# Earlier query loads, spaced recurrence loads and an earlier closing in a two-layer block

## Chip, core and metric

The kernel runs on one core of a Trainium2 chip. The metric is device time in microseconds for one execution of the whole program, about 92,000 instructions, of which one part is changed here.

## What is computed

A first block (gated delta rule beside a dilated attention, then a feed-forward part) gives x. Then two layers of a second block follow, on 256 context rows and 1024 rows of x, 1280 in all, with 1024 channels. A layer is, cut to what matters:

```python
h = x * (1 + scale) + shift                       # context rows have their own scale and shift
u, gates, q, k, v, nq, nk, nv = split(h @ w_in)
# recurrence: six heads of 64 x 64 state, one pass forward and one backward over the rows
S = S * w - (S @ kk) b^T + v k^T ;  y = S @ r
yr = group_norm(y_f + y_b) + bonus
ya = softmax(q k^T) v                             # six query heads on two key heads, all 1280 keys
yn = softmax([nq nk_window^T + bias, nq nk_ctx^T]) [nv_window, nv_ctx]     # four heads, local
x = layer_norm(alpha * x + gate * (concat(yr, ya, yn) * silu(gates)) @ w_out)
```

In the first layer the context rows are updated as well; in the last they aren't, so the attentions and the closing product have 8 tiles of 128 rows instead of 10. Products in the dense parts are made of three fp32r matmuls of high and low halves (L243 to L245).

## The kernel before

A layer has four parts: `front` (projections and the recurrence's factors), `stage` (the recurrence, both attentions and the gates' product), `finish` (closing product with w_out2, residual and layer norm), and the transposes for the next layer. The change lies in `stage` and `finish`.

In `stage` the order of work on TensorE, VectorE, ScalarE and GpSimd is written out by a planner, `Timeline`, and fixed in `tc.manual_schedule` for these four engines. Each stream of work is a generator. It yields a phase ("-" for work off TensorE; "F", "V", "B", "Q" for matmuls of one kind), a delay, the time from which it may go on, and the PSUM places that it wants. `Timeline.spend` adds up estimated durations, a DMA at 2 us plus its bytes; `run` takes, at each step, the stream that is due, smaller rank first. SP, whose queue issues all loads and stores, isn't among the engines of the manual schedule: its order is made by the scheduler, which issues a load once its buffer is free. On every engine instructions run in the order of its queue.

The streams of the stage:

- `scan` (rank 0): ten steps of the recurrence, each of two sub-steps with four products, each sub-step waiting for the one before. It needs the three preparations of its step. After a step it calls `launch(s + 2)`.
- `prep` (rank 1 + s * 0.05), one for each step and pair of heads, thirty a layer. It takes one of four tickets, loads `bk` (2 DMAs), `G` and `SK` (4 each), multiplies, then solves a triangular system in `tri_inverse2`: a small tensor `wC` goes out to `wD` (L423), comes back copied over the partitions as `wR` (L425, 512 KB), GpSimd runs 30 short instructions on it (L436, L438) and TensorE finishes (L449 to L485).
- `end` (rank 2): group norm of a finished pair of row blocks, and the store to `ydr` (L2022). The blocks of step 9 are the outermost of the sequence, those of step 6 the innermost (tiles 5 and 6).
- the attentions (ranks 3 and 4): `jobs` yields one job for a tile of 128 queries and a pair of heads, 30 + 20 of them in layer 0 and 24 + 16 in layer 1. For each, `query` loads four pieces of 32 KB into `qraw` (L2059, one buffer), casts them on ScalarE to `qst` (L2101) and subtracts on VectorE (L2104). Then `scores` multiplies (L687) and drains each bank on VectorE (L691), `soft` exponentiates (L648), `values` transposes (L723), copies (L727) and multiplies (L744), `put` stores.
- the gates' product ahead of them, tiles `gth` and `go` (L1538 to L1540).

`stage` runs the planner until all ends are done (`done.done`) and the third set of keys is there. Then the two pools on the right, E and W, which hold the recurrence's tiles and y, are closed, and `Closing` opens pools there. `Closing.loads` brings w_out2 in eight pieces (L2214), each cast on ScalarE (L2221) and subtracted on VectorE or GpSimd (L2223). The planner then runs dry. `finish` goes over the tiles in order; for each it loads the gates and `ydr`, multiplies (L2248), splits into `yh` and `yl` (L153, L154), multiplies with the weights (L243 to L245) and makes the norm.

Of the kernel before, what the change touches and what calls it, by code (L numbers as in the profile page):

```python
# [71 lines left out]
    return c  # L72


ALONE = {"a": FULL[2] + FULL[1] + FULL[0], "t": FULL[3] + FULL[5] + FULL[6], "pv": FULL[4] + FULL[7]}


class K:
# [547 lines left out]
def attend_rounds(k, rounds, wk, jobs, width, bufs):  # L626
# [7 lines left out]

    def load():
        for job in jobs(state):
            if isinstance(job, str):
                yield job
                continue
            loaded.append(job)  # L640
            state.todo += 1
            while loaded:
                yield WAIT
        state.more = False
# [117 lines left out]
D = 1024  # L762
# [536 lines left out]
D = 1024  # L1299
# [209 lines left out]
def gates(k, tl, I, l, last, dn, sets, cols, gp, hT, L):  # L1509

    nc = k.nc
    state = type("State", (), {"sets": 0, "done": False})()

    def weights():
        for i in (2, 3):
            sets.append((yield from dn.steps(cols(i), eng=nc.vector, go=lambda: state.sets > i - 2)))

    def products():
        for j in range(8):
            while len(sets) <= j // 2:  # L1520
                yield WAIT
            hi, lo = sets[j // 2]
            c = slice(j % 2 * 128, j % 2 * 128 + 128)
            for t0, n in LAT if last else SEG:
                for a in (0, 4):
                    yield "F", 0.0, 0.0, () if a else ("a",)
                    if a == 0:
                        p = k.bank([128, 512], "a")[:, :n]
                    else:
                        tl.used.append(k.places["a"][(k.turn["a"] - 1) % len(k.places["a"])])  # L1530
                    for kk in range(a, a + 4):
                        h, m = hT.at(kk, t0, n)
                        nc.tensor.matmul(p, lhsT=hi[:, kk, c], rhs=h, start=kk == 0, stop=False)
                        nc.tensor.matmul(p, lhsT=hi[:, kk, c], rhs=m, start=False, stop=False)
                        nc.tensor.matmul(p, lhsT=lo[:, kk, c], rhs=h, start=False, stop=kk == 7)
                th = gp.tile([128, 512], F32, tag="gth", name="gth", bufs=2)[:, :n]
                o = gp.tile([128, 512], F32, tag="go", name="go", bufs=2)[:, :n]
                nc.scalar.activation(th, p, AF.Tanh, scale=0.5)  # L1538
                nc.vector.scalar_tensor_tensor(o, th, 1.0, p, ALU.add, ALU.mult)
                nc.sync.dma_start(L.gates[:, j, t0:t0 + n], o)  # L1540
            state.sets = (j + 1) // 2
        state.done = True

    return weights(), products(), state


# [262 lines left out]
class Homes:  # L1809
# [3 lines left out]
    FIRST = {"SK00", "SK01", "G00", "G01", "AB0", "betok0", "wF0", "wS", "wC"} | {  # L1813
        f"{nm}{i}" for nm in ("bk", "A", "wB", "wR", "wX16", "wY16") for i in range(2)}

    def __init__(self, first):
        self.first, self.last = first, None

    def tile(self, shape, dtype, tag, name, bufs=1):
        return (self.first if tag in self.FIRST else self.last).tile(shape, dtype, tag=tag, name=name, bufs=bufs)  # L1820


def rwkv(k, rounds, wk, l, last, L):
# [42 lines left out]
    def prep(s, pr):  # L1866
        a = s % NS
        f, b = fwd[s], bwd[s]
        sk, g = SK[a], G[a]
        while not tickets:  # L1870
            yield WAIT
        ticket = tickets.pop(0)
# [40 lines left out]
    def scan():  # L1913
        for s in range(10):
# [69 lines left out]
            if want(s) and not first(s):  # L1984
                o = y.pop(group(s))
                for pr in range(3):
                    rounds.add(end(o[:, pr], pr, group(s)), 2, ended)

    def blocks(ap, g):

# [32 lines left out]

    done = [0] * 10
    tickets = [0, 1]
    state = type("State", (), {"ends": 0, "done": False})()

    def ended(_):
        state.ends += 1
# [22 lines left out]
def attention(k, rounds, I, kp, gp, l, last, L):  # L2052
# [20 lines left out]
    have = type("State", (), {"keys": 0})()  # L2073
    early = gp.tile([128, 2, NT], F32, name="early")
    for h in range(2):
        both(early[:, h], sets[0][h])
# [1 line left out]
    def keys(n):  # L2078
# [12 lines left out]
            yield "-"  # L2091
        have.keys += 1

    def query(srcs):

        raw = wk.tile([128, 2, 128], F32, tag="qraw", name="qraw", bufs=1)
        for h, src in enumerate(srcs):
            both(raw[:, h], src)
        yield "-"
        q = wk.tile([128, 2, 128], F32R, tag="qst", name="qst", bufs=3)  # L2100
        nc.scalar.copy(q, raw)  # L2101
        yield "-"
        lo = slice(64, 128)
        nc.vector.tensor_tensor(q[lo], raw[lo], q[lo].bitcast(F32), ALU.subtract)  # L2104
        yield "-"
        return q

# [1 line left out]
        return lambda h, a, n: [(q[:, h], t[:, first + a:first + a + n]) for t in KT[h]]  # L2109

    def put(j, ts_):
        return lambda yo: nc.sync.dma_start(L.ydr[:, j, ts_], yo)

    def tiles():
        for t in range(2 if last else 0, 10):
# [2 lines left out]
    def jobs(state):  # L2118
        def values(c0):
            v = wk.tile([128, 10, 128], F32, tag="nav", name="nav", bufs=2)  # L2120
            nc.sync.dma_start(v, L.nv[:, :, c0:c0 + 128])
            return v

        v = values(0)

        rounds.read()
        rounds.landed = 0.0
        for j in range(3):
            for t, ts_ in tiles():
                nk = NT if t >= 2 else CTX  # L2130
                q = yield from query([L.gqk[h * 64:h * 64 + 64, j, ts_] for h in range(2)])
                yield ([(nk, score(q), None)],
                       [(b * 128, lambda h, b=b, v=v: v[:, b, h * 64:h * 64 + 64]) for b in range(nk // 128)],
                       put(3 + j, ts_))
        for p in range(2):
# [10 lines left out]
            for t, ts_ in tiles():  # L2146
                if t >= 2:
# [13 lines left out]
                q = yield from query([L.nqk[h * 64:h * 64 + 64, p, ts_] for h in range(2)])  # L2161
# [31 lines left out]
class Closing:  # L2193


    def __init__(self, k, tc, I, l):
        self.pools = ExitStack()
        self.wr, self.wa, self.wb = (self.pools.enter_context(
            tc.tile_pool(name=f"{n}{l}", bufs=1, reuse_waits="tile", side="right")) for n in ("fr", "fa", "fb"))
        self.dn, self.ws = Dense(k, [self.wa, self.wb, self.wb, self.wb], self.wr, raws=2), [None] * 4  # L2200
        self.ap = I["w_out2"][l]

    def loads(self):
# [15 lines left out]
        for n, (i, a) in enumerate(parts):  # L2219
# [4 lines left out]
            if n < 4:  # L2224
                fetch()


def finish(k, tc, I, l, last, L, M, src, dst, done, cl):

    nc = k.nc  # L2230
    pool = lambda name, side: tc.tile_pool(name=f"{name}{l}", bufs=1, reuse_waits="tile", side=side)
    with cl.pools, pool("fy", "right") as wy, pool("fo", "left") as wk:
        dn, ws = cl.dn, cl.ws
        rows = None
        gate = wy.tile([128, 2, D], F32, name="gaterows")
        for v in range(2):
            nc.sync.dma_start(gate[:, v], M.gate[l][v:v + 1].to_broadcast([128, D]))
        for t in range(2 if last else 0, 10):
            ts_ = slice(t * 128, t * 128 + 128)

            y = []
            for o, e in ((3, 8), (0, 3)):
                n = e - o
                yr = wy.tile([128, n, 128], F32, tag=f"yr{o}", name="yr", bufs=2)
                gt = wy.tile([128, n, 128], F32, tag=f"gt{o}", name="gt", bufs=1)
                nc.sync.dma_start(gt, L.gates[:, o:e, ts_])
                nc.sync.dma_start(yr, L.ydr[:, o:e, ts_])
                nc.vector.scalar_tensor_tensor(yr, yr, 0.5, gt, ALU.mult, ALU.mult)  # L2248
                yh = wy.tile([128, n, 128], F32R, tag=f"yh{o}", name="yh", bufs=2)
                yl = wy.tile([128, n, 128], F32R, tag=f"yl{o}", name="yl", bufs=2)  # L2250
                k.split(yh, yl, yr)
                y.append((o, n, yh, yl))
# [91 lines left out]
def stage(k, tc, I, l, last, dn, hT, hps, L, weights):  # L2344
# [6 lines left out]
    with second:  # L2351
        ep = second.enter_context(pool("E", "right"))
        with ExitStack() as st:
            dn = Dense(k, [st.enter_context(pool(n, "right")) for n in ("ga", "gb")], st.enter_context(pool("gr", "right")), raws=2)
            cols = lambda i: [(I["w_in2"][l][:, 2688 + i * 256:2944 + i * 256], 0)]
            sets = [dn.load(cols(i), eng=nc.vector) for i in range(2)]
            k.places = SECOND
            gp = st.enter_context(pool("GT", "right"))
            man = tc.manual_schedule(engines={e.engine for e in (nc.tensor, nc.vector, nc.scalar, nc.gpsimd)})
            man.__enter__()  # L2360
            tl, homes = Timeline(k), Homes(ep)
            loads, products, gate = gates(k, tl, I, l, last, dn, sets, cols, gp, hT, L)
# [6 lines left out]
            ap = hps.enter_context(pool("A", "left"))  # L2369
            convert(ap)  # L2370
        homes.last = second.enter_context(pool("W", "right"))
        attend()
        go()
        tl.run(lambda: done.done and have.keys == 3)
    k.places = ALONE
    cl = Closing(k, tc, I, l)
    tl.add(cl.loads(), 8)
    tl.run()
    tl.close()
    man.__exit__(None, None, None)  # L2380
# [174 lines left out]
```

## Time and profile before

| | us |
|---|---|
| median of 3 runs | 4414.95 (4407.27 to 4433.86) |
| the profiled execution | 4414.57 |
| its span, first to last instruction | 4412.8 |
| TensorE busy | 3949.0 (89%) |
| GpSimd busy | 1699.5 (39%) |
| VectorE busy | 2166.8 (49%) |
| ScalarE busy | 1448.3 (33%) |

The page gives the busy time of each engine; the windows view gives it for a stretch, with the clock that TensorE was granted in it (1.00 is full speed) and the share of the 16 DMA engines. The waits view names for each waiting line the line that released it last. A row of the timeline is one instruction, or several alike, with the idle time of its engine just before it and what ended that. Where a short instruction waits in an engine's queue, all behind it wait too, so the name at the end of a wait is often not its cause.

### The profile page before, as it was taken

What the parts mean: (1) busy time and instruction counts of PE and PEld (TensorE: products, weight loads), DVE (VectorE), ACT (ScalarE), POOL (GpSimd) and SP (SyncE); (2) the same over time, 40 slices, a digit from 0 to 9 for tenths busy, and PEclk for the clock granted to TensorE, in tenths of its full rate; (3) what the DMA queues carried; (4) which work ended last, traced back from release to release, by engine and by line L of the source; (5) the groups of instructions that cost most, each with busy time, mean ns of one, the idle gap of its engine ahead of it and who ended that gap; (6) DMA issues with size and microseconds to landing.
All of it is one profiled execution on the core that took longest, in us unless ns stands there. A gap on an engine that the chain in (4) does not pass through costs nothing. (4 is left out here: it accounts for less than half of the span.)

```text
span 4412.8 us, 91628 instructions
## 1 busy us (share of the span) xinstructions
PE 3949.0 (89%) x36914; PEld 3200.0 (73%) x36914; DVE 2166.8 (49%) x4701; ACT 1448.3 (33%) x2831; POOL 1699.5 (39%) x3201
## 2 busy tenths in 40 slices
PE   8989998989999989899869898988989987898878
PEld 6767777967888867578747776778767866676658
DVE  5633332499221155664235555557566424554546
ACT  4244443321111132221125554442222114554341
POOL 2444333433232254342223444336444224434424
PEclk9999999999999989889979999999889998999889
DMA  3343224354111133453232334354345333324434
GB/s 112 117 131 88 82 74 131 127 162 151 44 46 50 43 120 114 152 179 95 81 102 63 74 73 109 91 157 144 114 156 177 104 98 81 76 64 100 100 111 138
DMA packets 523961, 466.87 MB, mean 106 GB/s; under 512 B 66416, under 2 KB 448656, under 8 KB 523408
## 3 DMA queue, kind: packets, MB, share of 16 engines
q1 hardware_dynamic: 523536, 461.02, 35.7%
q8 instruction: 289, 4.73, 0.4%
q14 instruction: 136, 1.11, 0.1%
HBM read 330.43 MB, written 130.43 MB: 104 GB/s over the span
## 5 line engine op out<-in xcount | busy, mean ns | idle before, releaser
L154 POOL TENSOR_TENSOR wlo<-wraw,whi 128x1024 fp32r<-128x1024 f32 (+3 forms) x134 | 318.9, 2395 | 565.1 <-ACT whi L153 513.1
L436 POOL TENSOR_TENSOR wY<-wR,wX 128x60 f32<-128x60 f32 (+5 forms) x900 | 233.3, 259 | 405.2 <-DMA wR<-wD 353.0
L153 ACT CAST whi<-wraw 128x1024 fp32r<-128x1024 f32 (+3 forms) x164 | 156.9, 989 | 372.5 <-PE bank L245 162.8
L691 DVE CUSTOM_DVE_ANT_0 S<-bank,zero 128x256 f32<-128x256 f32 (+1 forms) x372 | 204.5, 558 | 151.4 <-PE bank L687 149.4
L245 PE MATMUL bank<-h2T,wlo 128*128 128x512 f32 x704 | 278.5, 397 | 0.0
L244 PE MATMUL bank<-h2T,whi 128*128 128x512 f32 x704 | 278.0, 395 | 0.0
L243 PE MATMUL bank<-h2T,whi 128*128 128x512 f32 x704 | 275.6, 394 | 0.3 <-ACT h2T L785 0.3
L727 ACT COPY PT<-bank 128x512 f32<-128x512 f32 x346 | 201.7, 584 | 222.4 <-PE bank L723 221.6
L243 PE MATMUL bank<-whi,yh 128*128 128x256 f32 x832 | 240.5, 289 | 31.7 <-ACT yh L153 31.7
L438 POOL TENSOR_TENSOR wX<-wX,wY 128x60 f32<-128x60 f32 (+5 forms) x900 | 239.1, 266 | 70.5
L723 PE MATMUL bank<-cst,S 128*128 128x128 f32 x1416 | 238.4, 292 | 23.5 <-ACT PT L727 14.6
L744 PE MATMUL bank<-PT,nav 128*64 128x128 f32 (+1 forms) x2832 | 242.8, 294 | 16.5 <-ACT PT L727 16.1
L245 PE MATMUL bank<-whi,yl 128*128 128x256 f32 x832 | 238.9, 288 | 0.5 <-POOL yl L154 0.5
L244 PE MATMUL bank<-wlo,yh 128*128 128x256 f32 x832 | 239.2, 288 | 0.0
L744 PEld LDWEIGHTS bank<-PT,nav 128*64 128x64 f32 (+1 forms) x2832 | 154.4, 141 | 86.8 <-issue 55.3
L415 POOL TENSOR_TENSOR wB<-A,cst 128x256 f32<-128x256 f32 x60 | 45.2, 753 | 446.6 <-DVE A L1889 446.5
L723 PEld LDWEIGHTS bank<-cst,S 128*128 128x128 f32 x1416 | 164.1, 146 | 62.8 <-ACT PT L727 26.2
L648 ACT ACTIVATE S<-S,mx 128x1280 f32<-128x1280 f32 (+3 forms) x180 | 202.7, 1127 | 9.1 <-DVE mx L695 6.4
L243 PE MATMUL bank<-hT,whi 128*128 128x512 f32 x464 | 190.4, 410 | 9.1 <-ACT sqkv L131 6.7
L244 PE MATMUL bank<-hT,whi 128*128 128x512 f32 x464 | 187.3, 404 | 0.0
L243 PEld LDWEIGHTS bank<-whi,yh 128*128 128x128 f32 x832 | 162.5, 195 | 33.2 <-ACT yh L153 32.9
L245 PE MATMUL bank<-hT,wlo 128*128 128x512 f32 x464 | 186.2, 402 | 0.0
(467 smaller groups left out, 10919.3 us busy)
## 6 DMA issues: line engine op xcount, KB each, us to landing
wraw<-in_w_in SPq DMA_DIRECT2D x86, 512.0 KB
wR<-wD SPq DMA_DIRECT2D x60, 512.0 KB
wm<-in_w_mod SPq DMA_DIRECT2D x96, 256.0 KB
X<-R SPq DMA_DIRECT2D x12, 1280.0 KB
G<-gt SPq DMA_DIRECT2D x24, 640.0 KB
bk<-bk SPq DMA_DIRECT2D x24, 640.0 KB
bk<-bk SPq DMA_DIRECT2D x120, 128.0 KB
G<-G SPq DMA_DIRECT2D x240, 64.0 KB
```

What stands on the lines that cost most here:

```text
L153: self.nc.scalar.copy(hi, raw)
L154: (eng or self.nc.gpsimd).tensor_tensor(lo, raw, hi.bitcast(F32), ALU.subtract)
L243: nc.tensor.matmul(p, lhsT=lh, rhs=rh, start=kk == 0, stop=False)
L244: nc.tensor.matmul(p, lhsT=lh, rhs=rl, start=False, stop=False)
L245: nc.tensor.matmul(p, lhsT=ll, rhs=rh, start=False, stop=kk == n - 1)
L436: eng.tensor_tensor(t, custom(R, i * 64 + i + 1, [((15 - 2 * i) * 64 + 31 - i, 2), (16, 2), (1, n)]), custom(x, i, [(47 - 2 * i, 2), (16, ...
L438: eng.tensor_tensor(o, o, t, ALU.subtract)
L648: nc.scalar.activation(s[:, :total], s[:, :total], AF.Exp, bias=mx[:, 5:6], accum_out=mx[:, 6:7])
L691: nc.vector.tensor_tensor_reduce(out=s[:, c0:c0 + n], in0=p[:, c0 % 512:c0 % 512 + n], in1=b, scale=1.0, scalar=-3.0e38, op0=ALU.add, op1= ...
L723: nc.tensor.transpose(pt[:rows[i], i], P[h][0][:, c0:c0 + rows[i]], k.ident)
L727: nc.scalar.copy(t[:, :full], pt[:, :full])
L744: nc.tensor.matmul(pv[h * 64:h * 64 + 64, 0], lhsT=V, rhs=t[:V.shape[0], i], start=seen[h] == 1, stop=seen[h] == n)
```

## The change

- `query` no longer loads. `sources` lists all query tiles of the layer in the order of the jobs; `ask` loads the next one into `qraw`, which has two buffers, and notes when the planner takes it to have landed. Two are asked for at the start; each query asks for the next but one after its subtraction. The first queries of the second attention are so asked for ahead of its keys.
- `prep` of steps 1 to 9 yields a delay of 5 us times the number of its pair before it takes a ticket and loads.
- The planner's first run ends when the last scan has been placed (`done.scanned`) and the third set of keys is there, not when all ends are. The tiles `y`, `vv`, `gsq` and `hrs` move to the pool A on the left, which stays open; E and W are closed with ends still to come. `ALONE` gives up bank 0, and stands beside `SECOND` from then on.
- When the ends are done and the last attention has stored its first 2 (layer 0) or 5 (layer 1) tiles, the gates and `ydr` of the first two tiles of the closing are loaded, multiplied and split inside the stage (`Closing.first`, rank 7). The last layer's closing takes its tiles in the order 5, 6, 4, 7, 3, 8, 2, 9.
- The gates' tanh is written where the result goes; `go` has three buffers, `gth` is gone.

```diff
-ALONE = {"a": FULL[2] + FULL[1] + FULL[0], "t": FULL[3] + FULL[5] + FULL[6], "pv": FULL[4] + FULL[7]}
+ALONE = {"a": FULL[2] + FULL[1], "t": FULL[3] + FULL[5] + FULL[6], "pv": FULL[4] + FULL[7]}
...
-                th = gp.tile([128, 512], F32, tag="gth", name="gth", bufs=2)[:, :n]
-                o = gp.tile([128, 512], F32, tag="go", name="go", bufs=2)[:, :n]
-                nc.scalar.activation(th, p, AF.Tanh, scale=0.5)
-                nc.vector.scalar_tensor_tensor(o, th, 1.0, p, ALU.add, ALU.mult)
+                o = gp.tile([128, 512], F32, tag="go", name="go", bufs=3)[:, :n]
+                nc.scalar.activation(o, p, AF.Tanh, scale=0.5)
+                nc.vector.scalar_tensor_tensor(o, o, 1.0, p, ALU.add, ALU.mult)
...
+    ENDS = {"y", "vv", "gsq", "hrs"}
...
+        pool = self.first if tag in self.FIRST else self.ends if tag in self.ENDS else self.last
...
         sk, g = SK[a], G[a]
+        if s:
+            yield "-", 5.0 * pr
         while not tickets:
             yield WAIT
...
+        state.scanned = True
...
+    asked = []
+
+    def sources():
+        for src, j in [(L.gqk, j) for j in range(3)] + [(L.nqk, p) for p in range(2)]:
+            for _, ts_ in tiles():
+                yield [src[h * 64:h * 64 + 64, j, ts_] for h in range(2)]
+
+    def ask(srcs):
+
+        src = next(srcs, None)
+        if src is None:
+            return
+        raw = wk.tile([128, 2, 128], F32, tag="qraw", name="qraw", bufs=2)
+        rounds.read()
+        landed, rounds.landed = rounds.landed, 0.0
+        for h in range(2):
+            both(raw[:, h], src[h])
+        rounds.read()
+        asked.append((raw, rounds.landed))
+        rounds.landed = landed
+
     def query(srcs):
 
-        raw = wk.tile([128, 2, 128], F32, tag="qraw", name="qraw", bufs=1)
-        for h, src in enumerate(srcs):
-            both(raw[:, h], src)
-        yield "-"
+        raw, landed = asked.pop(0)
+        yield "-", 0.0, landed
         q = wk.tile([128, 2, 128], F32R, tag="qst", name="qst", bufs=3)
         nc.scalar.copy(q, raw)
         yield "-"
         lo = slice(64, 128)
         nc.vector.tensor_tensor(q[lo], raw[lo], q[lo].bitcast(F32), ALU.subtract)
+        ask(srcs)
         yield "-"
         return q
...
+        self.order = [5, 6, 4, 7, 3, 8, 2, 9] if last else list(range(10))
...
+    def mixed(self, t):
+
+        nc, wy = self.dn.k.nc, self.wy
+        ts_ = slice(t * 128, t * 128 + 128)
+        raws, y = [], []
+        for o, e in ((3, 8), (0, 3)):
+            n = e - o
+            yr = wy.tile([128, n, 128], F32, tag=f"yr{o}", name="yr", bufs=2)
+            gt = wy.tile([128, n, 128], F32, tag=f"gt{o}", name="gt", bufs=1)
+            nc.sync.dma_start(gt, self.L.gates[:, o:e, ts_])
+            nc.sync.dma_start(yr, self.L.ydr[:, o:e, ts_])
+            raws.append((o, n, yr, gt))
+        yield "-"
+        for o, n, yr, gt in raws:
+            nc.vector.scalar_tensor_tensor(yr, yr, 0.5, gt, ALU.mult, ALU.mult)
+            yield "-"
+            yh = wy.tile([128, n, 128], F32R, tag=f"yh{o}", name="yh", bufs=2)
+            yl = wy.tile([128, n, 128], F32R, tag=f"yl{o}", name="yl", bufs=2)
+            self.dn.k.split(yh, yl, yr)
+            y.append((o, n, yh, yl))
+        self.made.append(y)
+
+    def first(self):
+        for t in self.order[:2]:
+            yield from self.mixed(t)
...
-        for t in range(2 if last else 0, 10):
...
+        for n_, t in enumerate(cl.order):
+            if n_ > 1:
+                for _ in cl.mixed(t):
+                    pass
+            y = cl.made.pop(0)
...
-        tl.run(lambda: done.done and have.keys == 3)
-    k.places = ALONE
-    cl = Closing(k, tc, I, l)
+        tl.run(lambda: done.scanned and have.keys == 3)
+    k.places = {**SECOND, **ALONE}
+    cl = Closing(k, tc, I, l, L, last)
     tl.add(cl.loads(), 8)
+    tl.run(lambda: done.done and have.put >= (5 if last else 2))
+    tl.add(cl.first(), 7)
     tl.run()
```

## Rows read from the trace of the kernel before

**Rows 1.** The page: span, and busy time of each engine.

```profile
span 4412.8 us, 91628 instructions
PE 3949.0 (89%) x36914; PEld 3200.0 (73%) x36914; DVE 2166.8 (49%) x4701; ACT 1448.3 (33%) x2831; POOL 1699.5 (39%) x3201
```

**Rows 2.** Windows, all engines: length, busy (count) each, granted clock, DMA share, GB/s.

```profile
2230.00:2300.00 70.00, 32.96 (x575) 27.33 (x576) 26.48 (x76) 15.13 (x39) 18.86 (x65) 0.67 0.48 123
2300.00:2870.00 570.00, 509.50 (x9181) 405.63 (x9181) 300.10 (x1008) 277.45 (x604) 246.25 (x851) 0.94 0.33 81
...
3620.00:3670.00 50.00, 26.01 (x391) 20.16 (x392) 20.92 (x58) 11.33 (x24) 10.55 (x34) 0.66 0.48 126
3670.00:4250.00 580.00, 512.10 (x9062) 404.63 (x9061) 299.34 (x1009) 281.14 (x596) 248.87 (x874) 0.93 0.34 83
...
4272.00:4310.00 38.00, 12.46 (x78) 10.67 (x77) 14.39 (x17) 10.30 (x13) 16.53 (x12) 0.60 0.76 232
4310.00:4400.00 90.00, 87.83 (x732) 87.63 (x731) 62.67 (x80) 16.45 (x21) 44.48 (x35) 1.00 0.42 130
```

**Rows 3.** Waits of TensorE, 2225 to 2940: total us, times, longest us.

```profile
PE bank L687 <- DVE mx L691: 23.3, 3, 20.2
PE bank L1936 <- ACT W L1931: 13.8, 4, 7.7
PE bank L723 <- ACT PT L727: 11.6, 7, 3.5
...
PE bank L687 <- DVE qst L2104: 8.6, 3, 5.7
```

**Rows 4.** Waits of TensorE, 3617 to 4272.

```profile
PE bank L1885 <- DMA nab<-in_rpb: 10.4, 1, 10.4
PE bank L744 <- ACT PT L727: 8.4, 2, 4.3
...
PE bank L723 <- ACT S L648: 6.4, 1, 6.4
```

**Rows 5.** Timeline around 2260 to 2315 (start, us, engine, line, idle before), by engine.

```profile
2264.38 1.75 SPq L1877 DMA_DIRECT2D G<-G  x3
...
2282.14 0.59 SPq L1877 DMA_DIRECT2D G<-G  x1
...
2288.41 5.31 SPq L2059 DMA_DIRECT2D qraw<-gqk  x4
...
2295.83 0.40 ACT L2101 CAST qst<-qraw 128x256 fp32r<-128x256 f32 x1 [22.03 <-DMA qraw<-gqk]
...
2298.71 0.77 PE L687 MATMUL bank<-k0h,qst 128*128 128x512 f32 x1 [20.23 <-DVE mx L691]
...
2314.68 0.76 PE L149 MATMUL bank<-cst,wR 64*64 64x64 f32 x16
...
2292.05 0.29 POOL L436 TENSOR_TENSOR wY<-wR,wX 128x60 f32<-128x60 f32 x1 [13.61 <-DMA wR<-wD]
...
2301.68 0.61 POOL L440 TENSOR_TENSOR wR<-wX,cst 128x256 f32<-128x256 f32 x1
```

**Rows 6.** Timeline from the last end of layer 1 to the closing product.

```profile
4282.81 0.78 DVE L2021 SCALAR_TENSOR_TENSOR y<-y,gnb,vv 128x256 f32<-128x256 f32 x1
...
4287.88 2.94 ACT L2221 CAST whi<-wraw 128x1024 fp32r<-128x1024 f32 x3 [12.36 <-DMA ydr<-y]
...
4300.71 0.82 DVE L2248 SCALAR_TENSOR_TENSOR yr<-yr,gt 128x640 f32<-128x640 f32 x1 [5.00 <-DMA yr<-ydr]
...
4301.57 0.72 ACT L153 CAST yh<-yr 128x640 fp32r<-128x640 f32 x1 [9.47 <-DVE yr L2248]
...
4302.35 0.58 PE L243 MATMUL bank<-whi,yh 128*128 128x256 f32 x1 [20.17 <-ACT yh L153]
```

**Rows 7.** Waits of GpSimd, 3617 to 4272.

```profile
POOL wB L415 <- DVE A L1889: 163.8, 18, 22.1
```

**Rows 8.** Waits of SP's queue, 2225 to 2940.

```profile
SPq L2059 <- DVE qst L2104: 95.9, 24, 11.0
```

More of the change, by code (lines that the diff above doesn't have):

```diff
@@ L636, in load @@
         for job in jobs(state):
-            if isinstance(job, str):
+            if isinstance(job[0], str):
                 yield job
@@ L1814 @@
         f"{nm}{i}" for nm in ("bk", "A", "wB", "wR", "wX16", "wY16") for i in range(2)}
+    ENDS = {"y", "vv", "gsq", "hrs"}
     def __init__(self, first):
-        self.first, self.last = first, None
+        self.first, self.last, self.ends = first, None, None
     def tile(self, shape, dtype, tag, name, bufs=1):
-        return (self.first if tag in self.FIRST else self.last).tile(shape, dtype, tag=tag, name=name, bufs=bufs)
+        pool = self.first if tag in self.FIRST else self.ends if tag in self.ENDS else self.last
+        return pool.tile(shape, dtype, tag=tag, name=name, bufs=bufs)
 def rwkv(k, rounds, wk, l, last, L):
@@ L2025, in rwkv @@
     tickets = [0, 1]
-    state = type("State", (), {"ends": 0, "done": False})()
+    state = type("State", (), {"ends": 0, "done": False, "scanned": False})()
     def ended(_):
@@ L2072, in attention @@
     pend = []
-    have = type("State", (), {"keys": 0})()
+    have = type("State", (), {"keys": 0, "put": 0})()
     early = gp.tile([128, 2, NT], F32, name="early")
@@ L2111, in put, with store @@
     def put(j, ts_):
-        return lambda yo: nc.sync.dma_start(L.ydr[:, j, ts_], yo)
+        def store(yo):
+            nc.sync.dma_start(L.ydr[:, j, ts_], yo)
+            have.put += j == 7
+        return store
     def tiles():
@@ L2122, in values @@
             return v
+        srcs = sources()
+        for _ in range(2):
+            ask(srcs)
         v = values(0)
@@ L2130, in jobs @@
                 nk = NT if t >= 2 else CTX
-                q = yield from query([L.gqk[h * 64:h * 64 + 64, j, ts_] for h in range(2)])
+                q = yield from query(srcs)
                 yield ([(nk, score(q), None)],
@@ L2160, in jobs @@
                             bias.append(b)
-                q = yield from query([L.nqk[h * 64:h * 64 + 64, p, ts_] for h in range(2)])
+                q = yield from query(srcs)
                 if t < 2:
@@ L2193, with __init__ @@
 class Closing:
[L2196 to L2199, printed above, removed]
+    def __init__(self, k, tc, I, l, L, last):
+        self.pools, self.L = ExitStack(), L
+        self.wr, self.wa, self.wb, self.wy = (self.pools.enter_context(
+            tc.tile_pool(name=f"{n}{l}", bufs=1, reuse_waits="tile", side="right")) for n in ("fr", "fa", "fb", "fy"))
+        self.order = [5, 6, 4, 7, 3, 8, 2, 9] if last else list(range(10))
+        self.made = []
         self.dn, self.ws = Dense(k, [self.wa, self.wb, self.wb, self.wb], self.wr, raws=2), [None] * 4
@@ L2231, in finish @@
     pool = lambda name, side: tc.tile_pool(name=f"{name}{l}", bufs=1, reuse_waits="tile", side=side)
-    with cl.pools, pool("fy", "right") as wy, pool("fo", "left") as wk:
+    with cl.pools, pool("fo", "left") as wk:
         dn, ws = cl.dn, cl.ws
         rows = None
-        gate = wy.tile([128, 2, D], F32, name="gaterows")
+        gate = wk.tile([128, 2, D], F32, name="gaterows")
         for v in range(2):
             nc.sync.dma_start(gate[:, v], M.gate[l][v:v + 1].to_broadcast([128, D]))
-        for t in range(2 if last else 0, 10):
[L2239 to L2252, printed above, removed]
+        for n_, t in enumerate(cl.order):
[3 more added lines that the diff above has]
+            y = cl.made.pop(0)
             x = wk.tile([128, D], F32, tag="lx", name="lx", bufs=4)
@@ L2368, in stage @@
             hps.close()
-            ap = hps.enter_context(pool("A", "left"))
+            ap = homes.ends = hps.enter_context(pool("A", "left"))
             convert(ap)
```

## Prediction

> **What bounds the kernel now.** I read the page first, then busy times by stage, then TensorE's waits in the two stages that the change touches, then the timeline around the longest of them. The page says that TensorE is busy for 89% of the span [rows 1], so only its idle time and its time at the lower clock are to be had. The windows show where that lies: the stage of recurrence and attentions runs from about 2230 to 2940 in layer 0 and from 3620 to 4283 in layer 1. Its middles are 88 to 89% busy at a granted clock of 0.93 to 0.94; its starts are not: 33.0 us busy of 70 in layer 0 and 26.0 of 50 in layer 1, at 0.67 and 0.66; and between layer 1's stage and its closing product TensorE is busy 12.5 us of 38 [rows 2]. The closing product behind it is 98% busy [rows 2], so what is saved in front of it reaches the end.
>
> The waits view names the causes. In layer 0 TensorE waited 20.2 us once for L691, 13.8 us in four waits for the copy W, 11.6 us for PT and 8.6 us for the query's own subtraction [rows 3]; in layer 1 10.4, 8.4 and 6.4 us [rows 4]. The names are only the last link. The timeline of the 20.23 us gap shows the first: ScalarE stood 22.03 us at the query's cast L2101, because the four loads of that query were issued from 2288.41 on, and they stood in SP's queue behind 24 issues, all but one of them loads of G and SK for the next set, from 2264.38 to 2282.73 [rows 5]. That is 18.35 us, or 0.76 us for each, waits among them included. VectorE stood behind the cast, the score bank stayed full, TensorE stopped. The other waits counted here sit the same way behind a late cast; the 8.4 us group in layer 1 is two of them, 4.3 and 4.1 us.
>
> **Where the transfer itself is no cause.** From the end of the last of the four issues (2288.41 + 5.31 = 2293.72) to the cast it took 2.1 us [rows 5]. The lateness is in the queue. The Trainium skill, page "DMA: Bandwidth & Descriptors", section "Issuing engines are not separate DMA queues", says that the time a sequencer takes to initiate a DMA "is usually small relative to the DMA itself". By that rule a load one job ahead is early enough, and a second job of lead would bring nothing (the third rival); here the rows differ, 18.35 us of issues against 2.1 us of landing.
>
> **The change, part by part.**
>
> *Queries two jobs ahead.* The same four loads of 32 KB for each query, now with two buffers, asked for when the query two jobs earlier has been cast. Nothing is added on any engine. What it can remove is the idle time behind late casts: in layer 0 20.2 + 7.7 (the longest of the W group) + 11.6 + 8.6 = 48.1 us [rows 3], in layer 1 10.4 + 8.4 + 6.4 = 25.2 us [rows 4], 73.3 us together. How much comes back I take from the one gap that can be followed. Had TensorE gone on at 2278.5, it would have reached the first matmul that needs a solve, which stood at 2314.68, sixteen us of work later (2314.68 - 2298.71), at about 2294.5. The solve was ready at 2301.68 + 0.61 = 2302.3 [rows 5]. So 7.8 of the 20.2 us would turn into a wait for GpSimd, and 12.4 come back: 0.61 of it. Applied to all, 0.61 x 73.3 = 45 us. Bounds: nothing, where GpSimd or the scan is late next each time; 73 us, where it isn't.
>
> *Spaced loads.* A set's second and third pair load 5 and 10 us later in the planner's time. GpSimd waited 13.61 us, to 2292.05, for a wR whose path ran through the same queue [rows 5]; putting other issues between G and SK lets such a load out earlier. But SP's order isn't written by hand: SP is no engine of the manual schedule, so a load goes where its buffer is free, and the spacing may not survive. I price it at 0, from the 7.8 us above as a gain (it would make the first factor 1) to the fourth rival's loss. It adds no instruction; pairs were already apart by ten issues of 0.76 us, 7.6 us.
>
> *Clock.* At the stage starts 33.0 and 26.0 us of matmul time ran at 0.67 and 0.66 [rows 2]; at full clock the same would take 33.0 x 0.33 = 10.9 and 26.0 x 0.34 = 8.8 us less. The lower level (1.2 GHz) follows the gaps, so I take half, 10 us, between 0 and 19.7.
>
> *Closing weights and first operands.* In layer 1 TensorE stood 20.17 us before 4302.35, for the first operand yh [rows 6]. yr had come at 4300.71, because tile 2 waits for the recurrence's last stores, and ScalarE's third weight cast stood 12.36 us until a store of y had left memory that the weights reuse [rows 6]. Both go: y moves into the pool on the other side, and the last layer begins with tiles 5 and 6. What remains is the tail of the recurrence, whose last VectorE instruction ends at 4282.81 + 0.78 = 4283.59; behind it come one product (0.82 us) and one cast (0.72 us) [rows 6], 4285.1. Gain: 4302.35 - 4285.1 = 17.2 us. The eight weight casts of about 1 us and subtractions move into attention work where VectorE and ScalarE are about half busy (300 and 277 of 570) [rows 2]; without that cover ScalarE's 8 us would be paid. Bounds: 8 us, or 20.2. In layer 0 no such gap stands between the stages: 0.
>
> *The rest.* Scores lose bank 0 after the last scan, so they have two banks, as all through the stage; every wait of TensorE for such a bank but the one behind a cast comes to 23.3 - 20.2 = 3.1 us in all of layer 0 [rows 3], and the part of it here is set to 0. The gates' th buffer goes; the same two instructions remain. 0.
>
> *Sum.* 45 + 10 + 17.2 = 72 us. The profiled execution took 4414.57 us with a span of 4412.8, and the median of the runs is 4414.95, so they can be used alike. 4414.6 - 72 = 4342.
>
> **Rivals.**
>
> *All of it comes back* (chance 0.10): 73.3 + 19.7 + 20.2 = 113 us, 4301. For it speaks that the spacing also frees GpSimd's loads; against it that gaps seldom vanish without heirs.
>
> *The stall moves on* (0.20). VectorE's products A came late for GpSimd for 163.8 us in layer 1 [rows 7], and queries waited on SP for their own buffer 24 times, 95.9 us in layer 0 [rows 8], with wD and wR behind them; the second buffer keeps that wait in the queue. If only a quarter returns (18 us) with the closing's 17.2: 35 us, 4379.
>
> *The lead brings nothing* (0.08): the load is late wherever it stands, or one job would do. Only the closing is left: 4397. The 18.35 us speak against. The rule of the Trainium skill quoted above would have it so.
>
> *Slower* (0.07). The recurrence sets the end, and the third pair of each set is 10 us late. Nine sets follow the first in a layer, and two alternate, so a layer grows by 9 x 10 / 2 = 45 us, two by 90; less 17.2, and the starts' part of 45 (about 20), 4467. It speaks for it that in layer 1 the recurrence ends last, at 4283.59 [rows 6]; against it that pairs already load 7.6 us apart. It decides from the point where a scan waits for its third pair.
>
> **How the numbers follow.** The forecast has 0.55: 4342, alone perhaps 4315 to 4370. The range reaches to the moved stall and most of the third rival: 4300 to 4400; outside lie the slower case and a few in a hundred at either end. About 1% (44 us) is what a measurement of this kernel tells from no change: faster than 4371 are the forecast, the full gain and a third of the moved stall, 0.72; within 1% the rest of it and the third rival, 0.21; slower 0.07.
>
> **What would show it.** Waits of ScalarE at L2101's cast nearly gone in both layers (the 22.03 us one above all); the stage's starts above 0.8 busy at a higher clock; no gap over 5 us ahead of L243 in layer 1's closing product; no growth of TensorE's waits for solves (L149, L475, L481). Wrong it is if casts still wait more than half as long, if a wait for wR takes their place, or if the scans of layer 1 end later than 4265.

## The result and the profile after

The changed kernel takes 4357.6 us (median of 4 runs, 4353.97 to 4365.45) against 4419.8 us before: ratio 0.9862, 95% interval 0.9835 to 0.9888. The profiled execution took 4353.97 us. In the tables below three executions that lie far above all others, 8176.81 us of lead of one and 4922.47 and 9724.28 us of the kernel before beside it, enter no ratio. The page of the changed kernel, its span and busy times, to be held against [rows 1]:

```profile
span 4352.2 us, 91620 instructions
PE 3928.2 (90%) x36914; PEld 3184.2 (73%) x36914; DVE 2170.0 (50%) x4701; ACT 1451.1 (33%) x2831; POOL 1698.6 (39%) x3201
```

Each engine has as many instructions as before; what went is idle time and time at the lower clock. To see where, cut both traces at three marks: the first copy W of each layer's recurrence, the first product of layer 1's closing, the end. Windows of the kernel before (length, then busy time and count of TensorE, its weight loads, VectorE, ScalarE, GpSimd; granted clock, DMA share, GB/s):

```profile
2230.94:3626.44 1395.50, 1220.65 (x14199) 993.77 (x14199) 747.15 (x1692) 498.50 (x1002) 576.88 (x1285) 0.92 0.40 113
3626.44:4302.35 675.91, 562.24 (x9777) 443.43 (x9777) 337.72 (x1099) 307.75 (x644) 273.03 (x918) 0.90 0.35 89
4302.35:4409.50 107.15, 94.97 (x768) 94.47 (x768) 69.01 (x88) 20.29 (x25) 52.55 (x41) 0.93 0.45 138
```

The same three windows of the changed kernel, and the starts of its two stages and the middle of the first, which answer to [rows 2]:

```profile
2231.73:3606.06 1374.33, 1206.15 (x14199) 983.93 (x14199) 750.08 (x1692) 499.63 (x1003) 572.78 (x1285) 0.93 0.40 115
3606.06:4236.88 630.82, 558.69 (x9776) 440.11 (x9777) 333.61 (x1097) 305.99 (x642) 268.07 (x916) 0.93 0.37 91
4236.88:4348.90 112.02, 97.96 (x768) 96.40 (x768) 71.01 (x89) 23.29 (x28) 59.92 (x43) 0.93 0.50 164
...
2231.73:2300.00 68.27, 39.03 (x590) 30.69 (x592) 29.07 (x89) 17.66 (x44) 18.05 (x64) 0.73 0.47 122
2300.00:2870.00 570.00, 499.43 (x9130) 396.77 (x9124) 301.62 (x1019) 280.30 (x613) 244.32 (x852) 0.96 0.35 86
3606.06:3656.00 49.94, 42.05 (x564) 31.11 (x564) 28.67 (x84) 21.01 (x42) 12.70 (x44) 0.84 0.54 133
```

Idle is length less busy. From layer 0's first W to layer 1's: 21.2 us shorter, idle 174.9 to 168.2 (-6.7), busy -14.5. Layer 1's stage: 45.1 us shorter, idle 113.7 to 72.1 (-41.6), busy -3.6. The closing: 4.9 us longer, 3.0 of it busy time. With 0.8 us of later start that is the 60.6 us between the spans. Layer 1's start is now 0.84 busy at a clock of 0.84; layer 0's only 0.57 at 0.73.

Layer 0 gained little, and the waits say why. ScalarE's waits at the query cast before, layer 0 (total us, times, longest):

```profile
ACT qst L2101 <- DMA qraw<-gqk: 50.8, 8, 22.0
...
ACT qst L2101 <- DMA qraw<-nqk: 19.7, 8, 10.7
```

The changed kernel, layer 0: TensorE's longest waits, then ScalarE's at the cast:

```profile
PE bank L1889 <- DMA G<-G: 26.2, 7, 16.2
PE bank L723 <- ACT S L648: 10.2, 3, 7.4
PE bank L149 <- issue: 9.6, 1, 9.6
PE bank L149 <- POOL wR L440: 9.1, 3, 5.3
...
ACT qst L2125 <- DMA qraw<-nqk: 17.8, 5, 9.1
...
ACT qst L2125 <- DMA qraw<-gqk: 1.9, 2, 1.5
```

In the first attention (gqk) the late casts went; in the second (nqk) they stayed, 17.8 us of 19.7. The groups of [rows 3] went all the same: 23.3 us behind L691 became 0.5, 13.8 behind W became 2.7. G, which cost 4.0 us before, now costs 26.2; a wait for GpSimd's solve, which was not there, 9.1. In layer 1:

```profile
PE bank L149 <- POOL wR L440: 16.3, 3, 8.4
PE bank L1889 <- DMA G<-G: 6.2, 6, 2.2
...
PE bank L243 <- ACT yh L153: 3.8, 1, 3.8
...
ACT qst L2125 <- DMA qraw<-nqk: 2.8, 1, 2.8
```

The waits of [rows 4] are gone; the one for wR is the heir. The end of layer 1 in the timeline (start, us, engine, line, idle before), to be held against [rows 6]:

```profile
4233.71 0.48 DVE L2026 SCALAR_TENSOR_TENSOR y<-y,gnb,vv 128x256 f32<-128x256 f32 x1
...
4235.25 1.29 DVE L2275 SCALAR_TENSOR_TENSOR yr<-yr,gt 128x640 f32<-128x640 f32 x2
...
4236.10 1.14 ACT L153 CAST yh<-yr 128x640 fp32r<-128x640 f32 x2 [10.34 <-DVE yr L2275]
...
4236.88 0.58 PE L243 MATMUL bank<-whi,yh 128*128 128x256 f32 x1 [3.80 <-ACT yh L153]
...
4262.05 0.51 PE L243 MATMUL bank<-whi,yh 128*128 128x256 f32 x2 [1.57 <-ACT whi L2255]
```

From the end of the recurrence's last instruction to the closing's first it is 2.7 us (it was 18.8), and 3.8 us of idle are left of 20.17. A little is given back at 4262: the closing now overtakes its weight casts.

### The profile page after: what moved, and what is told of

The parts are those of the page before. It is cut to its first block, busy times and chain, and to the rows that moved or that the text cites. A ratio compares the mean times of both kernels' runs of the same rounds, so it can differ in the third digit from the quotient of the medians.

```text
span 4352.2 us, 91620 instructions
## 1 busy us (share of the span) xinstructions
PE 3928.2 (90%) x36914; PEld 3184.2 (73%) x36914; DVE 2170.0 (50%) x4701; ACT 1451.1 (33%) x2831; POOL 1698.6 (39%) x3201
## 4 chain that ended last, share of the span: by engine, by line
PE 30%; DMA 9%; DVE 7%; POOL 4%; issue 4%; ACT 2%; SPq 1%; POOLq 0%; DVEq 0%; ACTq 0%
PE bank L687 3%; PE bank L744 3%; PE bank L723 3%; DMA wR<-wD 3%; PE bank L243 2%; PE bank L244 2%; PE bank L245 2%; PE bank L1533 1%; PE bank L149 1%; PE bank L1535 1%; PE bank L1534 1%; POOL wX L438 1%; POOL wY L436 1%; DMA wD<-wC 1%; DMA X<-R 1%
## 5 line engine op out<-in xcount | busy, mean ns | idle before, releaser
L691 DVE CUSTOM_DVE_ANT_0 S<-bank,zero 128x256 f32<-128x256 f32 (+1 forms) x372 | 204.7, 558 | 173.6 <-PE bank L687 170.9
L243 PE MATMUL bank<-h2T,whi 128*128 128x512 f32 x704 | 275.9, 394 | 0.3 <-ACT h2T L785 0.3
L438 POOL TENSOR_TENSOR wX<-wX,wY 128x60 f32<-128x60 f32 (+5 forms) x900 | 237.6, 264 | 70.5
L243 PE MATMUL bank<-whi,yh 128*128 128x256 f32 x832 | 241.4, 291 | 17.7 <-ACT yh L153 16.1
L648 ACT ACTIVATE S<-S,mx 128x1280 f32<-128x1280 f32 (+3 forms) x180 | 202.9, 1127 | 10.3 <-DVE mx L695 8.5
L243 PE MATMUL bank<-hT,whi 128*128 128x512 f32 x464 | 190.1, 410 | 10.4 <-ACT sqkv L131 6.7
L1332 DVE CUSTOM_DVE_ANT_0 mj<-wm,cc 128x512 bf16<-128x512 f32 x192 | 179.3, 934 | 8.4 <-POOL cc L1320 3.2
```

Source lines behind the costliest of these rows:

```text
L243: nc.tensor.matmul(p, lhsT=lh, rhs=rh, start=kk == 0, stop=False)
L438: eng.tensor_tensor(o, o, t, ALU.subtract)
L648: nc.scalar.activation(s[:, :total], s[:, :total], AF.Exp, bias=mx[:, 5:6], accum_out=mx[:, 6:7])
L691: nc.vector.tensor_tensor_reduce(out=s[:, c0:c0 + n], in0=p[:, c0 % 512:c0 % 512 + n], in1=b, scale=1.0, scalar=-3.0e38, op0=ALU.add, op1= ...
L1332: nc.vector.tensor_tensor_reduce(out=j, in0=w, in1=cc[:, v, i * 512:i * 512 + 512], scale=1.0, scalar=0.0, op0=ALU.mult, op1=ALU.add, accu ...
```

## The experiments

All kernels, with the ratio to the kernel before on the same chip and the same three stretches of the profiled execution, in us. "W to W" holds layer 0's stage and closing and layer 1's front. Each stretch is of one execution, so the stretches need not add up to the medians: spacing 2.5, late solves and "all merged, spaced" were profiled in executions 17 to 19 us above theirs. The part ahead of the first W isn't in them: no edit is meant for it, and it varies (last section).

| kernel | median | ratio (95%) | layer 0, W to W | layer 1's stage | closing |
|---|---|---|---|---|---|
| before | 4409 to 4423 | 1 | 1395.5 | 675.9 | 107.2 |
| changed | 4357.6 | 0.9862 (0.9835 to 0.9888) | 1374.3 | 630.8 | 112.0 |
| queries alone (e1) | 4353.2 | 0.9875 (0.9845 to 0.9905) | 1367.2 | 636.1 | 106.4 |
| closing alone (e2) | 4391.8 | 0.9961 (0.9942 to 0.9979) | 1384.4 | 652.3 | 110.4 |
| spacing alone (e3) | 4377.4 | 0.9925 (0.9898 to 0.9953) | 1395.8 | 645.9 | 107.6 |
| all but spacing (e4) | 4327.4 | 0.9821 (0.9796 to 0.9846) | 1357.5 | 619.8 | 111.8 |
| spacing 2.5 (e5) | 4352.3 | 0.985 (0.9807 to 0.9893) | 1372.7 | 630.1 | 111.5 |
| spacing 10 (e6) | 4372.0 | 0.9886 (0.9848 to 0.9923) | 1357.9 | 643.5 | 112.5 |
| late solves (e7) | 4381.4 | 0.9897 (0.9844 to 0.995) | 1367.3 | 661.0 | 112.2 |
| merged preparations (e8) | 4302.3 | 0.9731 (0.9692 to 0.9771) | 1338.1 | 612.3 | 108.4 |
| merged alone (f1) | 4464.2 | 1.0105 (1.008 to 1.0131) | 1439.4 | 639.2 | 108.8 |
| all merged (f2) | 4404.8 | 0.9964 (0.9948 to 0.9979) | 1389.9 | 631.5 | 111.0 |
| lead of one (f3) | 4409.9 | 0.9975 (0.9961 to 0.9988) | 1401.3 | 627.8 | 111.8 |
| all merged, spaced (f4) | 4414.5 | 0.9987 (0.9967 to 1.0008) | 1394.6 | 638.7 | 112.2 |

**Each part alone, and all but one.** Theory A is the forecast's sum; S and C are its rivals.

```diff
 # e1, on the kernel before: sources, ask, qraw bufs=2, query as in the change; nothing else
-        raw = wk.tile([128, 2, 128], F32, tag="qraw", name="qraw", bufs=1)
+        raw, landed = asked.pop(0)
```

> The kernel before with the queries loaded two jobs ahead, and nothing else of the change. Theory A (the forecast's: the queries' lead is most of the gain and stands by itself): 40 to 55 us faster than before, ratio 0.988 to 0.991; waits at the query cast under 10 us in all in each layer. Rival S (without the spacing the preparations' burst of loads delays something else): 15 to 30 us faster, with new idle of PE behind G loads or behind the solves of GpSimd. Rival C (the closing part carries more than it was priced at): 25 to 40 us faster, and the closing alone brings the rest.

```diff
 # e2, on the kernel before: Closing.mixed, first and order, ENDS in pool A, scanned, ALONE, go bufs=3
+    tl.add(cl.first(), 7)
```

> The kernel before with the closing part alone: next weights and first operands from the last scan on, last layer's tiles in another order, four banks of layout kept; queries and preparations' loads as before. Theory A: 16 us faster, all of it at the gap before the first product of layer 1's closing (20.2 us before), nothing in layer 0. Rival C: 25 to 36 us faster, of which 10 between the first product of layer 0's closing and the start of layer 1's stage.

```diff
 # e3, on the kernel before
+        if s:
+            yield "-", 5.0 * pr
```

> The kernel before with the preparations' loads spaced by 5 us, alone. Theory A: within 5 us of before (priced at nothing: the planner moves the loads but the query cast still waits for its own load). Rival S: 10 to 25 us faster, because the query's load no longer stands behind a burst of 30 issues on SP; the wait at the query cast (22.0 us the longest, before) then falls without any lead.

```diff
 # e4, on the changed kernel
-        if s:
-            yield "-", 5.0 * pr
```

> The changed kernel without the spacing of the preparations' loads. Theory A: within 5 us of the changed kernel, ratio to before 0.985 to 0.988. Rival S: 15 to 30 us slower than the changed kernel, ratio 0.990 to 0.993. Third possibility, from the changed kernel's trace (PE waits 16.2 us for G of the second scan step in layer 0, loads issued late on SP): the spacing itself is what makes that load late; without it the wait is gone and the kernel is 5 to 16 us faster than the changed one.

Queries alone save 55 us (1.25%), as A says, though the casts wait more than its 10 us: 23.1 us in layer 0 and 23.8 in layer 1 (70.5 and 48.1 before). Their windows, W to W and layer 1's stage, to be held against the first two of the kernel before:

```profile
2246.09:3613.29 1367.20, 1201.83 (x14199) 981.47 (x14199) 752.82 (x1692) 499.13 (x1002) 574.82 (x1285) 0.93 0.40 115
3613.29:4249.35 636.06, 554.66 (x9777) 436.38 (x9777) 337.01 (x1099) 308.21 (x644) 272.84 (x918) 0.93 0.38 96
```

Idle time fell by 9.5 and 32.3 us. Closing alone saves 17 us (0.39%), A's size: its gap before L243 fell from 20.2 to 3.8 us. But layer 0 also became 11 us shorter, as C had it, for which A had nothing. Spacing is where A falls, and twice. Alone it saves 33 us (0.75%), all of it in layer 1's stage; and with the other two it costs: without it the kernel is 18 us faster by the ratios (0.9862 less 0.9821 of 4415, with intervals that overlap a little), 28 us by the stretches. The third possibility had that size, but not that cause: without spacing TensorE still waits for G of the second step. All but spacing, layer 0, then layer 1:

```profile
PE bank L1887 <- DMA G<-G: 25.8, 11, 13.7
...
PE bank L149 <- POOL wR L440: 3.5, 4, 1.5
...
PE bank L149 <- POOL wR L440: 3.7, 6, 1.1
```

What is gone is most of the wait for the solve: 9.1 and 16.3 us with the spacing, 3.5 and 3.7 without. That is 18.2 us, near the 20.2 us of idle time that went, but not layer by layer: the waits fell by 5.6 and 12.6, the idle time by 16.0 and 4.2. How the spacing alone helps stays open: S had the casts wait less, but with spacing alone the query casts of layer 0 still waited 40.0 and 17.6 us for their loads (50.8 and 19.7 before), and layer 0 gained nothing; those of layer 1, which gained 30 us, waited 50.4 (48.1 before).

**What the spacing costs.** Two sizes of it, and the same delay put elsewhere.

```diff
 # e5 and e6, on the changed kernel
-            yield "-", 5.0 * pr
+            yield "-", 2.5 * pr        # e6: 10.0 * pr
```

> The changed kernel with a spacing of 2.5 us instead of 5. The changed kernel without spacing measured 0.9821 of before, the changed kernel itself 0.9862. Theory P (each us of spacing starts the second and third solve of a step later, and PE then waits for their result: POOL wR 2.5 us without spacing, 24.8 us with 5): the cost grows with the spacing, here half of it, ratio 0.983 to 0.985. Rival R (any shift puts the planner's order elsewhere and its luck changes): no order between 0, 2.5, 5 and 10 us.

> The changed kernel with a spacing of 10 us. Theory P: 18 to 35 us slower than with 5, ratio 0.990 to 0.994, PE's waits for POOL wR over 40 us in both layers together. Rival R: anywhere between 0.980 and 0.992, with the waits for POOL wR not above the 24.8 us with 5.

```diff
 # e7, on the changed kernel without spacing: after the first products of prep
-        yield "-"
+        yield "-", 5.0 * pr if s else 0.0
         yield from tri_inverse2(k, wk, A, U[a][:, pr], ticket, nc.gpsimd)
```

> The changed kernel with the spacing taken from the loads and put before the solves instead: the loads and first products of the three preparations go at once, and the second and third solve of a step start 5 and 10 us later. Theory P (the lateness of the solves is the price): as slow as the changed kernel, ratio 0.985 to 0.988, with PE's waits for POOL wR of 15 us or more. Rival Q (the price is where the loads stand in SP's queue: the 16.2 us wait for G at the second step): as fast as without spacing, ratio 0.981 to 0.984.

TensorE's waits for the solve with a spacing of 2.5 us, layer 0 and layer 1:

```profile
PE bank L149 <- POOL wR L440: 8.7, 3, 3.9
...
PE bank L149 <- POOL wR L440: 15.2, 4, 7.9
```

With 10 us:

```profile
PE bank L149 <- POOL wR L440: 4.3, 2, 2.3
...
PE bank L149 <- POOL wR L440: 32.7, 6, 15.0
```

With late solves:

```profile
PE bank L149 <- POOL wR L440: 4.3, 4, 2.3
...
PE bank L149 <- POOL wR L440: 11.6, 4, 5.9
```

By the ratios the price follows the delay: 0.9821, 0.985, 0.9862 and 0.9886 with 0, 2.5, 5 and 10 us. Neighbours' intervals overlap; only 0 and 10 us stand apart (0.9846 against 0.9848), so "half the delay, half the cost" can't be told. With 10 us the time stayed below P's range, and the waits for wR, 37.0 us, under its 40.

In layer 1 the wait and the time go together. With 0, 2.5, 5 and 10 us the waits are 3.7, 15.2, 16.3 and 32.7, and the stage is 0, 10.3, 11.0 and 23.7 us longer than without. In layer 0 they don't. Its stage alone, up to its closing's first product, is 671.9, 683.2, 687.0 and 660.5 us long, with waits of 3.5, 8.7, 9.1 and 4.3: with 10 us it is shorter than with none. Layer 0's stage without spacing, then with 10 us:

```profile
2233.47:2905.34 671.87, 583.53 (x10211) 464.22 (x10211) 358.75 (x1222) 329.46 (x719) 275.72 (x924) 0.93 0.37 92
```

```profile
2247.77:2908.26 660.49, 581.05 (x10211) 463.13 (x10211) 360.28 (x1220) 327.66 (x719) 273.38 (x922) 0.94 0.37 92
```

So P's mechanism is borne out in layer 1 only. The planner lays its order anew with each delay: in layer 1's stage TensorE's order in the changed kernel leaves that of the kernel without spacing within the first fifty matmuls. How much of the price is this new order, R's luck, the runs don't separate.

Late solves measured 0.9897, and the interval (0.9844 to 0.995) holds P's range and none of Q's. So Q, the loads' place on SP, isn't the price by itself. But P isn't shown by this run: a late solve also holds its ticket through the delay, the waits for wR, 15.9 us, are fewer than the changed kernel's 25.4, and of the 41 us by which its layer 1 is longer than without any delay they make 7.9. Another 18.0 are busy time (its clock there was 0.90 against 0.94).

**Fewer issues on SP.** Each of 60 preparations, ten loads to six.

```diff
 # e8, on the changed kernel without spacing; two(): one DRAM pattern over both directions
-                nc.sync.dma_start(g[h][HS[h], pr, d * 2:d * 2 + 2], L.G[HS[h], pr, d, blk * 2:blk * 2 + 2])
-                nc.sync.dma_start(sk[h][HS[1 - h], pr, 0, d * 2:d * 2 + 2], L.vT[:, pr, h, blk * 2:blk * 2 + 2])
+            nc.sync.dma_start(g[h][HS[h], pr].rearrange("p (d c) x -> p d (c x)", d=2),
+                              two(lambda d, x: L.G[HS[h], pr, d, x * 2:x * 2 + 2], 256))
+            nc.sync.dma_start(sk[h][HS[1 - h], pr, 0].rearrange("p (d c) x -> p d (c x)", d=2),
+                              two(lambda d, x: L.vT[:, pr, h, x * 2:x * 2 + 2], 128))
```

> The changed kernel without spacing, and each preparation's ten loads made six: both directions of G, and of the transposed values, in one transfer each. In the trace without spacing a preparation's loads take 0.59 us of SP each, and PE waits 29 us in all for G. Theory (SP's issues are what makes G and queries late): the waits for G fall under 15 us and the time by 8 to 20 us against without spacing, ratio 0.978 to 0.980. Rival (the issues are hidden, and the wait for G is PE's order, set by a planner that takes 0.06 us for an issue): within 5 us, ratio 0.981 to 0.984.

4302 us, faster than either kernel: 0.9731 of before, 40 us under the kernel without spacing by the ratios, twice the most that was expected. But the cause in the expectation is wrong. Merged preparations, layer 0, then layer 1:

```profile
PE bank L1892 <- DMA G<-G: 26.8, 4, 13.8
...
POOL wY L436 <- DMA wR<-wD: 130.9, 25, 13.5
...
PE bank L1892 <- DMA G<-G: 8.9, 3, 5.0
...
POOL wY L436 <- DMA wR<-wD: 122.0, 26, 13.5
```

The waits for G didn't fall (25.8 and 8.2 us without merging). GpSimd's waits for wR, whose two transfers go through the same queue, fell from 148.6 and 129.2 to 130.9 and 122.0. TensorE's clock rose to 0.96 in both stages (0.93 and 0.94): of the 26.9 us by which W to W and layer 1's stage are shorter, 18.7 are busy time, and 8.2 idle time spread over many small waits. That fewer and larger loads save is shown; that it is by the shorter queue isn't, because TensorE's order is another here too.

**A merge too far.** All four ran on one chip.

```diff
 # f1 on the kernel before (with e8's merged loads), f2 on e8
     def both(out, src):
-        for i in range(2):
-            nc.sync.dma_start(out[i * 64:i * 64 + 64], src)
+        nc.sync.dma_start(out, bass.AP(tensor=src.tensor, offset=src.offset, ap=[[0, 2]] + [list(x) for x in src.ap]))
 # f3, on f2: one ask at the start instead of two
-        for _ in range(2):
-            ask(srcs)
+        ask(srcs)
 # f4, on f2: the spacing of 5.0 * pr again
```

> The kernel before with merged loads alone: six transfers for a preparation instead of ten, and two for a query instead of four (both halves of the partitions in one); queries as late as before, no spacing, no early closing. Theory L (what made the queries late is the length of SP's queue: 30 issues of 0.6 us for a step's preparations, four for a query): a large part of the lead's gain comes without any lead, 30 to 60 us faster, ratio 0.986 to 0.993, the longest wait at the query cast under 15 us (22.0 before). Rival (a query asked for in its own job is late whatever stands ahead of it: about 2 us landing and the cast's place): less than 20 us faster, ratio over 0.995.

> The changed kernel without spacing, with six transfers for a preparation and two for a query. With six and four it measured 0.9731 of before. Theory L: the 90 queries cost SP 0.6 us x 2 x 90 = 108 us less; waits for G (46 us in both layers with six and four) fall under 30 us, time 8 to 20 us under that, ratio 0.968 to 0.971. Rival: hidden, ratio 0.972 to 0.975.

> As all_merged, but queries loaded one job ahead instead of two. Theory L: with short queues one job (about 14 us of the stage a job) is enough, within 8 us of all_merged. Rival (the forecast's: the lead must cover the 18 us that a step's preparations take on SP): 15 to 30 us slower than all_merged, with waits at the query cast of 5 us and more.

> As all_merged, with the preparations' loads spaced by 5 us as in the changed kernel: on the same chip as all_merged, so that the price of the spacing is measured directly. Theory P (late solves): 15 to 30 us slower than all_merged, PE's waits for POOL wR over 15 us (6.0 in the kernel with six and four). Rival (the spacing's price came from the long queue): within 8 us of all_merged.

All merged is 100 us slower than merged preparations. `both` also loads the keys (`early`, `kraw`), and there it shows. Some 30 us of it are in layer 1's front alone (581.1 us from the closing to the first W, 551.3 in merged preparations), and the first W of layer 0, whose front does the same, comes 34 us later. The two stages are 49.5 us longer together; queries go through `both` too, but how much of this is theirs isn't shown. SP and TensorE in all merged, in layer 1's front:

```profile
3479.12 1.13 SPq L2066 DMA_DIRECT2D early<-gqk  x2
3480.29 9.78 SPq L202 DMA_DIRECT2D wraw<-in_w_in  x1
3490.17 5.31 SPq L1505 DMA_DIRECT2D nqk<-fo  x1
3495.53 9.39 SPq L202 DMA_DIRECT2D wraw<-in_w_in  x1
...
3514.31 0.58 PE L243 MATMUL bank<-hB,whi 128*128 128x256 f32 x1 [19.80 <-ACT fo L129]
```

The DMA busy share in tenths and the GB/s there, in 40 slices from 3478 to 3516:

```profile
DMA  0001111111111489511711111111169924110169
GB/s 16 0 0 27 49 54 54 54 54 54 49 49 54 83 264 200 97 54 61 273 58 54 54 54 49 49 54 54 54 152 281 146 57 161 42 39 12 19 164 316
```

And in merged preparations around the same loads, from 3420 to 3452:

```profile
DMA  9003899999899999920489279981040000170000
```

The same bytes, in two transfers instead of four, keep 0.1 of the 16 DMA engines busy instead of 0.9, at 54 GB/s, and what is issued behind them stands in SP's queue. The Trainium skill says so, page "DMA: Bandwidth & Descriptors", section "Rules for kernel authors": an outermost dimension smaller than 16, such as a leading zero-stride broadcast, confines the transfer to at most as many engines. Two of 16 is 0.125; the trace agrees. The merged G and SK have 64 partitions outermost: in merged preparations 12 of them were issued from 2285.7 on, at 0.6 us each as before, and 131 GB/s were moved from 2284 to 2296.

So f1 can't tell whether short queues do without the lead: it carries this loss. Lead and closing on top of it are worth 59 us (f1 to f2). One job of lead instead of two costs 5 us there, 0.9975 against 0.9964 with intervals that overlap, and the query casts waited 26.5 us in all against 53.4: one job would nearly have done with merged loads. With ten loads a preparation it wasn't run. The spacing's price, measured directly, is 10 us, 0.9987 against 0.9964, less than P's 15 to 30 and not clear of the noise (the intervals overlap from 0.9967 to 0.9979); the waits for the solve in layer 1 rose from 9.7 to 14.8 us. All merged, then all merged and spaced:

```profile
PE bank L149 <- POOL wR L440: 9.7, 3, 6.4
```

```profile
PE bank L149 <- POOL wR L440: 14.8, 2, 7.5
```

## Why the prediction was right, point by point

4342 was forecast, 4357.6 measured: inside 4300 to 4400 and inside the likeliest case's own 4315 to 4370. The cause, late queries, was right; that SP's long queue makes them late was read from one gap, and merged alone, which should have tested it, can't tell. That the total came so near is partly luck: the clock gave 8 us more than its term, the queries 13 and the closing 6 less.

- *Queries, 45 us.* 31.9 came back as idle time: 6.7 in layer 0, and in layer 1 the 41.6 less the closing's 16.4, 25.2. The factor of 0.61 was taken from one gap and put on all, and neither layer has it. In layer 1 as much as [rows 4]'s 25.2 us came back; in layer 0 0.14 of 48.1 did. Queries alone, where no spacing interferes, saved 55 us, just the 45 + 10 of the sum, but again not as it was added up: their 41.8 us of idle time are 0.20 of layer 0's 48.1 and 1.28 of layer 1's 25.2. In the gap that was followed, ten more issues stood between the 24 and the query, from 2282.82 to 2288.41.
- *Spacing, 0.* This step failed. The bounds were there (7.8 us of gain, the fourth rival's loss), and so was the mark: "if a wait for wR takes their place". It did, for 25.4 us (2.0 before). The price of 0 rested on the planner not deciding when a load goes. But the delay also moves the first products, which do stand in the planner's order, and with them the start of the solves. It cost 10 us directly measured, 18 to 28 between the kernels; alone it gained 33. The rival's mechanism, a late solve and TensorE waiting for it, is what layer 1 shows; its size, 45 us a layer, was far too large.
- *Clock, 10 us.* Busy time fell by 14.5 + 3.6 = 18.1, near the upper bound, but not at the starts alone, where it was priced: layer 0's start went only from 0.67 to 0.73 of the clock, and its middle, at 0.96 (0.94), took 499.4 us for 9130 matmuls instead of 509.5 for 9181 [rows 2].
- *Closing, 17.2 us.* 16.4 at the gap, less 4.9 in the closing itself: 11.5. The cover for the casts and the first operands' split isn't complete; about 5 us of waits now stand within the closing product (0.5 before). Layer 0, priced at 0, is 11 us shorter with the closing alone: its closing product now starts while attentions still run, at 2907.9 instead of 2928.9.
- *Sum.* 31.9 + 18.1 + 11.5 - 0.8 = 60.7 us, against 72 forecast.
- *Starts.* Above 0.8 in layer 1 (0.84), not in layer 0 (0.57): there the 16.2 us wait for G took the place of the 20.2 us one. Layer 1's last W was copied at 4214 and its last group norm done at 4234, well before 4265.
- *The rule of the Trainium skill* (page "DMA: Bandwidth & Descriptors", section "Issuing engines are not separate DMA queues"). That an issue is usually small beside its transfer, by which a lead would bring nothing, doesn't hold for a queue of thirty short ones: queries alone save 55 us. Its weaker form, that one job is enough, nearly holds with merged loads (f3); with the long queue no run shows it.

## What to carry to other kernels

A wait that vanishes leaves room for the next one in line: look up which load or solve is ready only just behind it, separately for each stage, before a share of one gap is put on all. Two edits against one cause don't add: spacing the loads and asking earlier were each good alone (33 and 55 us), and together the spacing cost 10 to 28 us. With the queries asked for earlier, issuing fewer, larger transfers gained 40 us where spacing the same issues lost, as long as the outermost dimension of each still spreads over all DMA engines. And where a planner lays the order, a small delay moves all that follows: look at more than one size of it, and at each layer, before one wait is called the price.

## What the runs showed that was not expected

The 54 GB/s transfers above, and this: the same instructions ahead of the stage took up to 23 us longer in some executions. Windows of 300 us early in the program, the changed kernel:

```profile
300.00:600.00 300.00, 285.84 (x2410) 222.34 (x2409) 109.53 (x355) 131.20 (x282) 115.63 (x243) 0.99 0.32 87
```

And spacing 2.5, which differs only 1,600 us later:

```profile
300.00:600.00 300.00, 287.06 (x2283) 222.66 (x2283) 105.05 (x339) 125.66 (x273) 107.85 (x237) 0.91 0.28 79
```

At 0.91 instead of 0.99 of the clock 127 fewer matmuls were done in the window, and the first W came at 2252.1 instead of 2231.7 (2254.5 in late solves). That is why single spans say less here than stretches cut at the same instructions, and medians of several runs.
